# Two buffers for the transposed q and k of a differential-attention layer, its weights in pieces of 512 columns

## The chip, the cores and the metric

The kernel runs on one core of one Trainium2 chip. The metric is the device time of one execution in microseconds (us), the median of several runs. A profiled execution gives the trace from which all rows below are read; its time axis starts at the span's start.

## The reference

The program is a two-layer trunk on 640 tokens (128 of context, 512 of latents) of 1024 features. Layer 0 runs multi-head latent attention beside bidirectional retention. Layer 1 runs **differential attention** (4 heads) beside a bidirectional **RWKV-7** time mixing (8 heads). Each layer is followed by a gated convolutional feed-forward block. The part that matters here, cut to its core:

```python
# layer 1, differential half (h: normalised input, 640 x 1024)
q, k, v = h @ w_q, h @ w_k, h @ w_v          # 512 columns each
q = rope(rms_norm(q) * gain_q); k = rope(rms_norm(k) * gain_k)   # per head of 64; no rotation of the context tokens
k, v = concat(cached_k, k), concat(cached_v, v)
w = softmax(q1 @ k1.T) - lam * softmax(q2 @ k2.T)                # two maps per head
o = w @ v
# layer 1, RWKV half: for each of 640 tokens, forward and backward
state = state * decay - (state @ kk) (kk * a) + v k
```

## The kernel before, in words

The scan of the RWKV half (`rwkv_scan`, from about 1043 us to 1504 us of the span) is built from a main and a background stream. The main stream consists of `pre(g)` (the decays, gates and key products of a group of 128 tokens in each of the two directions: tiles `wp`, `lp`, `am`, `th`, `bp`, `sa`, `sb`, `kt`, `hq`, `L`), `lb(g)` and `lc(g)` (the inverse of the triangular matrices of group g, in DVE's line L1902 and its neighbours, with a round trip through DRAM at L1908 to L1917: `xd<-X`, then `X<-xd`), and `steps(g, d)` (the state updates, `pa`, `SV`, `yp`). The background stream is `side_mix`: `odd_qkv`, which makes the q, k and v of the differential layer, and after it `diff_attn`, the attention. `weave` (L241) advances the streams by a table of numbers when the program is written out. A scheduler then puts each engine's instructions into one fixed order by its own estimate of when each can start; that order is final, and every engine works it off in sequence.

`odd_qkv` runs through six groups of 256 columns: two of q, two of k, two of v. Each group needs 1 MB of weights, `w`, fetched on the SP queue by `load(g)` (L1311). Its products are five tiles of 128 tokens, eight matrix products each, at L1325: 240 instructions, 480 records in the trace since each is done in two passes. A q or k tile is post-processed one group later by `post` (L1277): DVE scales it (L1287), POOL applies the gain (L1288), DVE and POOL rotate it (L1293 to L1297), PE transposes it into the tile `qtr` (L1303), ACT and DVE split the transposed tile into two parts, `pt` (L440 and L444, called at L1305), and two DMAs on the SP queue carry `pt` to DRAM (L1307: `dq<-pt` for q, `dk<-pt` for k). There are 20 such tiles. The tile `pt` has one buffer, the weights have three buffers of 1024 columns. All tiles of `odd_qkv` come from one pool of fixed size. At the end the 512 KB of cached keys are loaded into one such weight buffer (L1347), split into two others, and written to `dk` (L1352); the attention reads `dk` afterwards.

The SP queue issues DMAs in its fixed order. Where a DMA needs data or a buffer that is not there yet, the queue stands at it, and what is behind it waits as well.

Of the kernel before, what the change touches and what calls it, by code (L numbers as in the profile page):

```python
# [9 lines left out]
F32 = mybir.dt.float32  # L10
F32R = mybir.dt.float32r
# [6 lines left out]
D = 1024  # L18
# [86 lines left out]
def _consts3():  # L105
    """Head sums land in rows 32 p + i; the selectors bring rows 32 p + i and 32 p + 2 + i back to half i of tile p."""
# [103 lines left out]
"""How the streams of the layers are woven: background steps in each part of the scan, spans of layer 0."""  # L210
# [3 lines left out]
LAG = 4  # L214


class Side:
    """A background stream: its matrix products are issued behind the main streams' product of LAG events before."""
# [22 lines left out]
def weave(bg, rate, *parts):  # L241
    """Advance several emission streams together; each (generator, begin, end) spreads evenly over [begin, end]."""
    ev = []
    for i, (g, b, e) in enumerate(parts):
        n = NSTEP[g.__name__]
# [17 lines left out]
class Trunk:  # L263
# [116 lines left out]
    def setup_late(self):  # L380
        """The loads that nothing needs before the first products."""
# [174 lines left out]
    def ada_half(self, c0):  # L556
        """Eight chunks of layer 0's modulation, from pieces that the queue brings in this order."""
# [30 lines left out]
    def norm_mod(self, side):  # L588
        """Layer 0: rstd and x * rstd do not wait for the modulation."""
# [26 lines left out]
    def norm_begin(self, l, which, pool):  # L616
        """Open the next norm: every final x[k] is scaled by the modulation and split at once, its rstd is applied after the
        matrix product; two more columns carry the shifts through it."""
# [19 lines left out]
    def norm_end(self, us, rb):  # L638
        """Close the norm: the first three products run while the rstd is being worked out."""
# [17 lines left out]
    def fm_norm(self, h, u, rb, ps=None):  # L657
        """One output tile of the normalised product, into the padded columns of u."""
# [104 lines left out]
    def head_sums(self, sqs, stat, mmt, tile):  # L763
        """Per-head sums of four tiles of squares: [tokens, (token tile, tile, half)]."""
# [16 lines left out]
    def head_rows(self, r, mmt, tile):  # L781
        """The [tokens, (token tile, tile, half)] columns as rows of hi and lo parts."""
# [16 lines left out]
    def head_bcast(self, rows, p, mmt):  # L799
        """Tile p of the rows, spread over the features of its two heads."""  # L800
# [134 lines left out]
    def mla_cached(self, kr, ccs, D):  # L935
        """Keys and values of the cache, before the first products."""
# [39 lines left out]
    def mla_rows(self, src, dst, tt, g, gain, D, tr):  # L976
        """Four heads of 128 tokens, turned to rows of features."""
# [288 lines left out]
    def odd_qkv(self, D):  # L1266
        """Differential q, k, v from the stored h: one 256-column group at a time, its post-processing one group behind."""
        nc, a = self.nc, self.a
        with self.pool("qk", 1, "left") as qp, self.psum("qps", 2) as qps, self.psum("qtr") as qtr:
# [41 lines left out]
            def load(g):  # L1311
                w = [tile("w", 1024, 3) for _ in range(2)]
                for i in range(2):
                    nc.sync.dma_start(w[i], a["wb_tm"][g][:, i * 1024:i * 1024 + 1024])
# [799 lines left out]
```

## Time and profile before

| what | us |
|---|---|
| median of three runs | 2073.32 |
| the three runs | 2075.4, 2061.55, 2073.32 |
| span of the profiled execution | 2059.5 |
| PE busy in it | 1952.7 (95%) |
| DVE busy in it | 1253.8 (61%) |
| ACT busy in it | 887.3 (43%) |

Of the profiled execution only the span is listed, no separate run time; the shortest run is 2 us longer than this span, the median 13.8 us. The stretch in which `odd_qkv` and the main stream of the scan run side by side is 1043 us to 1232 us. In the rows a name stands for a tile, `out<-in`; what stands in brackets behind a row, as [3.67 <-POOL th L1824], is how long the engine was idle before it and which instruction ended that.

### The profile page before, as it was taken

The numbers are of one execution on the slowest core, as the hardware profiler recorded it, in microseconds if no ns is written. First come the engines' busy times: TensorE is split into PE (matmuls) and PEld (weight loads), VectorE is DVE, ScalarE is ACT, GpSimd is POOL, SyncE is SP. The second block draws the span as 40 slices with busy tenths as digits, with TensorE's granted clock in tenths as the row PEclk, the third lists the DMA queues.
The fourth block names the chain that finished last, engine by engine and source line by source line (L and its number), as shares of the span: only waits on it lengthen the run. The fifth ranks groups of instructions, "written<-read, shape, count | busy, mean of one in ns | idle before, by whom it ended". The sixth has DMA issues, their size and how long they took to land.

```text
span 2059.5 us, 36275 instructions
## 1 busy us (share of the span) xinstructions
PE 1952.7 (95%) x14376; PEld 1765.7 (86%) x14376; DVE 1253.8 (61%) x2752; ACT 887.3 (43%) x1680; POOL 186.5 (9%) x365
## 2 busy tenths in 40 slices
PE   6999999999999999999989897898779999999999
PEld 3998565999899899999978676777679999999999
DVE  6554657556456465577436856877667764656555
ACT  4433344334244243456333334667534542524343
POOL 1001000000000000000024332332110000000000
PEclk9999999999999999999989998979989999999999
DMA  8237344234543512143264554454453212122221
GB/s 323 67 109 242 105 134 163 89 104 147 181 153 116 192 62 83 60 151 104 83 207 100 109 161 120 100 116 96 100 200 106 77 58 92 60 85 67 77 63 71
DMA packets 190676, 243.60 MB, mean 118 GB/s; under 512 B 90730, under 2 KB 132970, under 8 KB 190508
## 3 DMA queue, kind: packets, MB, share of 16 engines
q1 hardware_dynamic: 184880, 225.87, 35.7%
q0 software_dynamic: 3904, 13.37, 2.2%
q8 instruction: 113, 1.85, 0.4%
q10 hardware_dynamic: 1724, 2.06, 0.3%
q14 instruction: 55, 0.45, 0.1%
HBM read 202.05 MB, written 39.21 MB: 117 GB/s over the span
## 4 chain that ended last, share of the span: by engine, by line
PE 81%; DVE 7%; DMA 6%; ACT 3%; issue 2%; POOL 1%; SPq 0%; ACTq 0%; DVEq 0%; POOLq 0%
PE mm L470 59%; PE qkv L1325 2%; PE ada L541 2%; PE rv L913 1%; PE pv L1130 1%; PE mm L1097 1%; DMA dk<-pt 1%; PE ptr L1120 1%; PE sc L1442 1%; DVE X L1902 1%; DVE tmp L1901 1%; DMA xd<-X 1%; DMA mq<-tr 1%; DMA raw<-ada 1%; PE mm L1098 1%
## 5 line engine op out<-in xcount | busy, mean ns | idle before, releaser
L414 ACT CAST hi<-raw 128x1024 fp32r<-128x1024 f32 (+4 forms) x212 | 195.9, 925 | 574.1 <-PE mm L470 528.6
L470 PE MATMUL mm<-hhi,hi 128*128 128x322 f32 x1648 | 381.0, 312 | 0.0
L470 PE MATMUL mm<-hlo,hi 128*128 128x322 f32 x1648 | 380.3, 311 | 0.0
L470 PE MATMUL mm<-hhi,lo 128*128 128x322 f32 x1648 | 380.1, 311 | 0.0
L470 PEld LDWEIGHTS mm<-hhi,hi 128*128 128x128 f32 x1648 | 278.3, 189 | 8.7 <-issue 6.7
L470 PEld LDWEIGHTS mm<-hlo,hi 128*128 128x128 f32 x1648 | 279.5, 190 | 0.0
L470 PEld LDWEIGHTS mm<-hhi,lo 128*128 128x128 f32 x1648 | 278.6, 189 | 0.0
L415 DVE TENSOR_TENSOR lo<-raw,hi 128x1024 fp32r<-128x1024 f32 (+4 forms) x212 | 226.1, 1067 | 58.7 <-ACT hi L414 36.0
L672 DVE SCALAR_TENSOR_TENSOR x<-mm,ada,x 128x512 f32<-128x512 f32 (+1 forms) x176 | 88.7, 545 | 176.1 <-PE mm L470 175.9
L470 PE MATMUL mm<-ahi,hi 128*128 128x320 f32 x704 | 161.7, 311 | 0.0
L470 PE MATMUL mm<-ahi,lo 128*128 128x320 f32 x704 | 160.7, 309 | 0.0
L470 PE MATMUL mm<-alo,hi 128*128 128x320 f32 x704 | 160.3, 309 | 0.0
L663 DVE COPY shv<-mm 128x2 f32<-128x2 f32 x103 | 16.3, 159 | 207.9 <-PE mm L470 207.9
L470 PEld LDWEIGHTS mm<-ahi,hi 128*128 128x128 f32 x704 | 117.1, 188 | 12.0 <-ACT hi L414 10.1
L1325 PE MATMUL qkv<-w,x 128*128 128x256 f32 x480 | 118.9, 402 | 0.1
L470 PEld LDWEIGHTS mm<-ahi,lo 128*128 128x128 f32 x704 | 117.8, 188 | 0.0
L470 PEld LDWEIGHTS mm<-alo,hi 128*128 128x128 f32 x704 | 117.6, 188 | 0.0
L666 ACT ACTIVATE u<-u,shv 128x128 f32<-128x128 f32 (+1 forms) x176 | 90.3, 557 | 48.8 <-DVE u L665 47.0
L734 DVE SCALAR_TENSOR_TENSOR ac<-u,vt,ac 128x642 f32<-128x642 f32 x88 | 78.0, 887 | 52.5 <-ACT ac L732 52.3
L1325 PEld LDWEIGHTS qkv<-w,x 128*128 128x128 f32 x480 | 94.0, 201 | 17.0 <-issue 1.7
L732 ACT ACTIVATE ac<-u,vt 128x642 f32<-128x642 f32 x88 | 81.3, 925 | 2.8
L665 DVE TENSOR_TENSOR u<-mm,rb 128x128 f32<-128x128 f32 (+1 forms) x176 | 77.3, 481 | 2.5 <-ACT rb L650 2.5
(419 smaller groups left out, 3351.3 us busy)
## 6 DMA issues: line engine op xcount, KB each, us to landing
raw<-ada SPq DMA_DIRECT2D x96, 512.0 KB, 4.6
raw<-up SPq DMA_DIRECT2D x88, 512.0 KB, 3.5
raw<-down SPq DMA_DIRECT2D x32, 384.0 KB, 3.1
raw<-down SPq DMA_DIRECT2D x32, 320.0 KB, 2.8
fs<-df SPq DMA_DIRECT2D x10, 832.0 KB, 5.2
raw<-wb_fm SPq DMA_DIRECT2D x15, 512.0 KB, 3.5
w<-wb_tm SPq DMA_DIRECT2D x12, 512.0 KB, 4.5
raw<-wa_fm SPq DMA_DIRECT2D x11, 512.0 KB, 4.3
```

What stands on the lines that cost most here:

```text
L414: nc.scalar.copy(hi, t)
L415: nc.vector.tensor_tensor(lo, t, hi.bitcast(F32), op=OP.subtract)
L470: nc.tensor.matmul(ps[:, c0 + b:c0 + e], wt[:, ws], at[:, b:e], start=first and j == 0, stop=last and j == 2)
L541: nc.tensor.matmul(ps[32 * j:32 * j + 32, :], self.cs[:, k, :], pieces[j // 2][:, (j % 2) * 512:(j % 2) * 512 + 512], start=k == 0, stop=k ...
L665: nc.vector.tensor_tensor(u[:, o], ps[:, s], rb[:, s], op=OP.mult)
L666: nc.scalar.activation(u[:, o], u[:, o], AF.Identity, bias=sh[:, c:c + 1])
L672: nc.vector.scalar_tensor_tensor(x[:, s], ps[:, s], self.ada_v(l, part, m, c), x[:, s], op0=OP.mult, op1=OP.add)
L732: nc.scalar.activation(ac, u[:, 1:643], AF.Identity, scale=cv[:, 1, f:f + 1], bias=self.vec(f"cb{l}", f))
L734: nc.vector.scalar_tensor_tensor(ac, u[:, 0:642], cv[:, 0, f:f + 1], ac, op0=OP.mult, op1=OP.add)
L913: nc.tensor.matmul(ps[:, :272], at[:, ts], wt[:, k * 272:k * 272 + 272], start=n == 0, stop=n == 23)
L1097: nc.tensor.matmul(sc[:, 0:512], q, kT[:, 0:4], start=True, stop=True)
L1325: nc.tensor.matmul(ps, h[k][:, t * 128:t * 128 + 128], w[k // 4][:, k % 4 * 256:k % 4 * 256 + 256], start=k == 0, stop=k == 7)
```

## The change

The tile `pt` gets two buffers. To make room in the pool of unchanged size, the weights of a group come in four pieces of 512 columns (256 KB) in five buffers, where they came in two of 1024 (512 KB) in three. The product at L1325 picks the piece by `k // 2`. The cached keys are loaded, split and written in two halves of 512 columns, one behind the other. The pool's use is the same to the word: 3 x 1024 + 512 before, 5 x 512 + 2 x 512 after. Comments were removed as well, which changes no instruction. The core of the diff:

```diff
-                    pts = tile("pt", 512, 1, F32R).rearrange("p (n x) -> p n x", n=2)
+                    pts = tile("pt", 512, 2, F32R).rearrange("p (n x) -> p n x", n=2)
...
             def load(g):
-                w = [tile("w", 1024, 3) for _ in range(2)]
-                for i in range(2):
-                    nc.sync.dma_start(w[i], a["wb_tm"][g][:, i * 1024:i * 1024 + 1024])
+                w = [tile("w", 512, 5) for _ in range(4)]
+                for i in range(4):
+                    nc.sync.dma_start(w[i], a["wb_tm"][g][:, i * 512:i * 512 + 512])
                 return w
...
-                        nc.tensor.matmul(ps, h[k][:, t * 128:t * 128 + 128], w[k // 4][:, k % 4 * 256:k % 4 * 256 + 256], start=k == 0, stop=k == 7)
+                        nc.tensor.matmul(ps, h[k][:, t * 128:t * 128 + 128], w[k // 2][:, k % 2 * 256:k % 2 * 256 + 256], start=k == 0, stop=k == 7)
...
-            kc = tile("w", 1024, 3)
-            ks = [tile("w", 1024, 3, F32R) for _ in range(2)]
-            nc.sync.dma_start(kc, a["dkc"])
-            self.split_to(*ks, kc)
-            for i in range(2):
-                for c in range(2):
-                    for g in range(2):
+            for g in range(2):
+                kc = tile("w", 512, 5)
+                ks = [tile("w", 512, 5, F32R) for _ in range(2)]
+                nc.sync.dma_start(kc, a["dkc"][:, g * 512:g * 512 + 512])
+                self.split_to(*ks, kc)
+                for i in range(2):
+                    for c in range(2):
```

The scheduler lays out the engines' orders anew. PE has the same instructions; between the first product of `odd_qkv` and the products `lf` of L1943 of the first half of `lb(0)`/`lc(0)` their order differs, behind that it is nearly the same.

The first place is PE's order at the third `bp` (the product behind `th` of L1824, of the second group of `pre`). Numbers behind names count tiles. Before:

```order
L1303 MATMUL qtr_10931<-ident,raw_10705 128x128 x2
L1325 MATMUL qkv_10992<-w_10710,x_77 128x256
L1325 MATMUL qkv_10992<-w_10710,x_79 128x256
L1325 MATMUL qkv_10992<-w_10710,x_81 128x256
L1325 MATMUL qkv_10992<-w_10710,x_83 128x256
L1325 MATMUL qkv_10992<-w_10711,x_85 128x256
L1325 MATMUL qkv_10992<-w_10711,x_87 128x256
L1325 MATMUL qkv_10992<-w_10711,x_89 128x256
L1325 MATMUL qkv_10992<-w_10711,x_91 128x256
L1827 MATMUL bp_11296<-th_11267,rkb 32x128 x4
L1858 MATMUL sa_11344<-kr_11314,kb_11313 128x128 x4
L1859 MATMUL sb_11345<-kr_11314,kb_11313 128x128 x4
```

Now:

```order
L1325 MATMUL qkv_11232<-w_10960,x_77 128x256
L1325 MATMUL qkv_11232<-w_10960,x_79 128x256
L1325 MATMUL qkv_11232<-w_10961,x_81 128x256
L1325 MATMUL qkv_11232<-w_10961,x_83 128x256
L1325 MATMUL qkv_11232<-w_10962,x_85 128x256
L1325 MATMUL qkv_11232<-w_10962,x_87 128x256
L1325 MATMUL qkv_11232<-w_10963,x_89 128x256
L1325 MATMUL qkv_11232<-w_10963,x_91 128x256
L1303 MATMUL qtr_11148<-ident,raw_10955 128x128 x2
L1827 MATMUL bp_11320<-th_11291,rkb 32x128 x4
L1858 MATMUL sa_11368<-kr_11338,kb_11337 128x128 x4
L1325 MATMUL qkv_11260<-w_10960,x_77 128x256
```

Before, the product stands behind the 17th tile of products of `odd_qkv` and the transposes of the 10th tile of q and k; now it stands behind the 22nd tile of products and the 15th tile's transposes. The RWKV rows move back by 50 instructions there, the rows of `odd_qkv` move forward. From this pass's `wp` to its `bp` PE has 32 products of L1325 to do, where it had 24; from `bp` to the next `kt` 26, where it had 8.

The second place is PE's order at the fourth `wp` (the start of `pre(1)`'s second direction). Now:

```order
L1325 MATMUL qkv_11500<-w_11162,x_81 128x256
L1325 MATMUL qkv_11500<-w_11162,x_83 128x256
L1303 MATMUL qtr_11360<-ident,raw_11085 128x128 x2
L1791 MATMUL wp_11517<-wup_10315,wx_10343 128x512
L1325 MATMUL qkv_11500<-w_11163,x_85 128x256
L1325 MATMUL qkv_11500<-w_11163,x_87 128x256
L1303 MATMUL qtr_11428<-ident,raw_11123 128x128 x2
L1800 MATMUL lp_11528<-c_3608,lw_11519 128x128 x4
L1815 MATMUL am_11546<-fs_11272,aup 128x128 x4
L1325 MATMUL qkv_11500<-w_11164,x_89 128x256
L1325 MATMUL qkv_11500<-w_11164,x_91 128x256
```

Before:

```order
L1303 MATMUL qtr_11032<-ident,raw_10804 128x128 x2
L1873 MATMUL kt_11479<-ident,kb_11313 128x64 x4
L1873 MATMUL kt_11479<-ident,kb_11381 128x64 x4
L1791 MATMUL wp_11493<-wup_10315,wx_10343 128x512
L1325 MATMUL qkv_11108<-w_10710,x_77 128x256
L1325 MATMUL qkv_11108<-w_10710,x_79 128x256
L1325 MATMUL qkv_11108<-w_10710,x_81 128x256
L1325 MATMUL qkv_11108<-w_10710,x_83 128x256
```

The chain `wp`, `lp`, `am` stood in the fourth group of products and now stands in the sixth, the last; a product on that group's third piece, `w_11163`, now stands between `wp` and `lp`. From this `wp` to its `bp` there are 6 products of L1325, where there were 24.

The third place is the SP queue where the inverse of `lb(0)` makes its round trip (`xd`, `zd`, `X`, `zb`). Before:

```order
L1314 DMA w_10945<-wb_tm 128x1024
L1909 DMA xd_11591<-X_11286 128x32x16
L1908 DMA zd_11592<-ZI_11589 128x16x32
L1314 DMA w_11141<-wb_tm 128x1024
L1307 DMA dk<-pt_11076 64x4x128 x2
L1917 DMA X_11599<-xd_11591 32x2x256 x2
L1913 DMA zb_10336<-zd_11592 32x16x32 x4
```

Now:

```order
L1909 DMA xd_11615<-X_11310 128x32x16
L1908 DMA zd_11616<-ZI_11613 128x16x32
L1314 DMA w_11162<-wb_tm 128x512
L1338 DMA dv<-raw_11422 128x256
L1917 DMA X_11623<-xd_11615 32x2x256
L1307 DMA dk<-pt_11238 64x4x128
L1314 DMA w_11163<-wb_tm 128x512
L1307 DMA dk<-pt_11238 64x4x128
L1314 DMA w_11164<-wb_tm 128x512
```

Before, the first half of the last group's weights, `w_11141`, stood ahead of the reload `X<-xd`, and its second half 12 rows behind it. Now the second piece stands ahead of the first `X` DMA, the third and the fourth, `w_11163` and `w_11164`, right behind it, with a `dk<-pt` before each. Further up in the queue the second half of `LI<-ld`, the input of `lb(0)`, now stands behind the DMAs of the tenth `pt`; before, both halves stood ahead of the seventh's.

## Rows read from the trace of the kernel before

**Rows 1.** The page: span, engines' busy time, the products of L1325 (busy, mean ns | idle before).
```profile
span 2059.5 us, 36275 instructions
...
PE 1952.7 (95%) x14376; PEld 1765.7 (86%) x14376; DVE 1253.8 (61%) x2752; ACT 887.3 (43%) x1680; POOL 186.5 (9%) x365
...
L1325 PE MATMUL qkv<-w,x 128*128 128x256 f32 x480 | 118.9, 402 | 0.1
```

**Rows 2.** Waits from 1043 to 1240 us: total us, times, longest.
```profile
ACT pt L440 <- DMA dq<-pt: 13.9, 6, 3.7
ACT pt L440 <- DMA dk<-pt: 13.0, 5, 4.0
```

**Rows 3.** Chain of waits from 1043 to 1240 us: shares, one piece.
```profile
by line: PE qkv L1325 24.2%; DMA dk<-pt 12.9%; issue 7.6%; DMA dq<-pt 5.8%; DVE X L1902 3.6%; DVE tmp L1901 3.2%; SPq L1307 2.6%; DVE pt L444 2.5%; ACT pt L440 2.3%; PE wp L1791 2.1%; PE kt L1873 2.0%; DVE kb L1849 1.9%; DVE raw L1287 1.9%;
...
1064.75 7.10 PE qkv L1325 x32
```

**Rows 4.** Timeline of ACT: two of the 20 pt splits, the steps' first SV.
```profile
1101.08 0.37 ACT L440 CAST pt<-qtr 128x256 fp32r<-128x256 f32 x1 [3.68 <-DMA dq<-pt]
...
1140.57 0.37 ACT L440 CAST pt<-qtr 128x256 fp32r<-128x256 f32 x1 [2.33 <-DMA dq<-pt]
...
1232.71 0.78 ACT L1982 ACTIVATE SV<-pa 64x256 f32<-64x256 f32 x2 [0.78 <-PE pa L1980]
```

**Rows 5.** Windows of 20 us: busy us by engine, then PEclk, DMA share, GB/s.
```profile
1080.00:1100.00 20.00, 19.95 (x132) 16.23 (x129) 10.86 (x27) 6.55 (x17) 8.87 (x12) 1.00 0.13 27
...
1140.00:1160.00 20.00, 11.98 (x73) 9.49 (x71) 19.72 (x55) 5.04 (x13) 9.83 (x12) 0.83 0.22 63
1160.00:1180.00 20.00, 20.00 (x98) 16.78 (x97) 13.30 (x43) 9.33 (x24) 4.89 (x10) 0.91 0.72 126
...
1200.00:1220.00 20.00, 18.39 (x188) 13.95 (x189) 5.39 (x19) 7.13 (x19) 0.96 (x3) 0.87 0.52 126
```

**Rows 6.** Timeline of PE around its two longest pauses and at L1943.
```profile
1137.40 0.44 PE L1303 MATMUL qtr<-ident,raw 128*128 128x128 f32 x2 [0.78 <-DVE pt L444]
1137.68 3.62 PE L1325 MATMUL qkv<-w,x 128*128 128x256 f32 x16
1144.96 0.43 PE L1827 MATMUL bp<-th,rkb 128*32 128x128 f32 x8 [3.67 <-POOL th L1824]
...
1147.33 5.00 PE L1325 MATMUL qkv<-w,x 128*128 128x256 f32 x16
...
1154.30 0.41 PE L1303 MATMUL qtr<-ident,raw 128*128 128x128 f32 x2 [0.75 <-DVE raw L1297]
...
1159.17 1.12 PE L1873 MATMUL kt<-ident,kb 64*128 64x64 f32 x8 [3.60 <-DVE hq L1863]
1160.21 5.16 PE L1325 MATMUL qkv<-w,x 128*128 128x256 f32 x15
...
1211.10 0.60 PE L1943 MATMUL lf<-zb,tt 32*32 32x32 f32 x26
```

**Rows 7.** Timeline of the SP queue: issue start, issue time.
```profile
1125.96 1.13 SPq L1887 DMA_DIRECT2D LI<-ld  x2
...
1169.69 0.39 SPq L1909 DMA_DIRECT2D xd<-X  x1
...
1177.52 1.27 SPq L1917 DMA_DIRECT2D X<-xd  x2
...
1248.25 0.38 SPq L1909 DMA_DIRECT2D xd<-X  x1
```

**Rows 8.** DMA issues from 1040 to 1250 us: count, KB each, median to landing.
```profile
w<-wb_tm SPq DMA_DIRECT2D x12, 512.0 KB, 4.5
...
dk<-pt SPq DMA_DIRECT2D x20, 128.0 KB, 2.6
...
LI<-ld SPq DMA_DIRECT2D x4, 256.0 KB, 4.2
...
w<-dkc SPq DMA_DIRECT2D x1, 512.0 KB, 5.8
```

More of the change, by code (lines that the diff above doesn't have):

```diff
@@ L1344, in odd_qkv @@
                 w = wn
-            kc = tile("w", 1024, 3)
-            ks = [tile("w", 1024, 3, F32R) for _ in range(2)]
-            nc.sync.dma_start(kc, a["dkc"])
-            self.split_to(*ks, kc)
-            for i in range(2):
-                for c in range(2):
-                    for g in range(2):
+            for g in range(2):
[5 more added lines that the diff above has]
+                    for c in range(2):
                         nc.sync.dma_start(D["k"][g, c, 2 * i:2 * i + 2, :, 5:7].rearrange("h d t k -> d h (t k)"),
-                                          ks[i][64 * c:64 * c + 64, g * 512:g * 512 + 512].bitcast(F32).rearrange("p (h x) -> p h x", h=2))
+                                          ks[i][64 * c:64 * c + 64].bitcast(F32).rearrange("p (h x) -> p h x", h=2))
             yield
```

## The prediction, made before the changed kernel was run

> **What bounds the kernel now.** I read the page first. PE is busy for 1952.7 us, 95% of a span of 2059.5 us [rows 1]. So whatever the change does, it counts only where PE itself stands still or runs at its lower clock. The buffer in question is seen next, in the waits of the stretch in which it is used. ACT, which writes the first half of `pt`, waits 13.9 us for the landing of `dq<-pt` and 13.0 us for that of `dk<-pt`, eleven waits in all [rows 2]. ACT's timeline shows what such a wait is: the split could begin, but the only buffer is still being read by the DMA, which takes 2.6 us from issue to landing [rows 4, 8]. In this stretch's own chain of waits those landings stand with 12.9% and 5.8% [rows 3]. That looks like 26.9 us to be had. The reader should now ask who waits for ACT.
>
> The windows answer. In 1080 to 1100 us PE is busy for 19.95 of 20 us, though the most of ACT's wait of 3.68 us lies inside, and in 1160 to 1180 us for 20.00 [rows 4, 5]. Between one `pt` and the next, PE has the products of L1325 to do: 32 records in 7.10 us, or 0.222 us each, so the 480 records are some 106 us [rows 3]. They cover most of the waits. PE stands still in one window only, 1140 to 1160 us, with 11.98 us busy, where DVE is full with 19.72 us; a smaller loss is in 1200 to 1220 us, with 18.39 us [rows 5]. PE's timeline gives the two long pauses: 3.67 us before `bp`, until POOL's `th`, and 3.60 us before `kt`, until DVE's `hq` [rows 6]. Neither of them is a wait for `pt`; both belong to the RWKV stream, whose DVE work is in the same queue as the work on q and k. After each pause the granted clock is at the lower level for a while: PEclk is 0.83 and 0.91 in these two windows and 1.00 before [rows 5], and 16 products take 5.00 us where 16 took 3.62 us just ahead [rows 6].
>
> **The change, part by part.** *The second `pt` buffer* removes the eleven waits on ACT. By itself that gives PE nothing where it is full. What it moves is the order: the rows of `odd_qkv` go forward, those of `pre` back. From the `wp` of the pass with the first pause to its `bp` PE now has 32 products, where it had 24: eight more, of two records each, 3.6 us, the length of the pause. From there to the `kt` with the second pause it has 26 where it had 8, 8.0 us more against a pause of 3.60 us. I take both as gone, and two short ones between them, before transposes that waited for DVE: 3.67 + 3.60 + 0.78 + 0.75 = 8.8 us. The half-clock products go with them: 5.00 - 3.62 = 1.38 us for the 16 after the first pause, and 5.16 - 15 x 0.222 = 1.83 us for the 15 after the second [rows 3, 6]. Together that is **12 us gained**. The bounds: nothing, if the pauses turn up at another place, since DVE's work is the same; and 16 us, if PE has no pause left at all, which is 8.0 + 1.6 us of idle time in the two windows and the clock's missing shares, 0.17 x 12 + 0.09 x 20 + 0.13 x 18.4 = 6.2 us [rows 5].
>
> *What is late next.* Since `pre` now runs later and `odd_qkv` earlier, two new waits can come. The first is on the last group's weights. On the SP queue the third and fourth piece stand behind the reload `X<-xd`, which waits until the result of `lb(0)` has been in DRAM. In the trace `xd` is issued at 1169.69 us and `X` at 1177.52 us, 7.8 us later, and the queue stands for that time [rows 7]. One `dk<-pt` issue follows, so the third piece is issued about 1.2 us after `X` and lands by the row of the nearest size, 256 KB in 4.2 us [rows 8], that is some 13 us after `xd`. PE wants it before `lp` of the last `pre` pass. When is that? The `lf` of L1943 stands at 1211.10 us [rows 6]; less 12 us it is at 1199 us; between lie 20 products of 0.444 us, 8.9 us, and about as much of the RWKV stream's (an estimate, from its rows in the same place before), so PE is there at about 1181 us. With `xd` as before the piece lands at 1183 us, and PE waits 2 us. But `lb(0)` begins later: the second half of its input, issued at 1125.96 us before [rows 7], now stands behind the tenth `pt`, which was split at 1140.57 us [rows 4], at best some 2.3 us earlier without its wait. So the input comes up to 12 us later. DVE is freer by then, because work on q and k has been done early, and I take `xd` to be 3 us later: 1173 us, the piece at 1186 us, and **5 us lost**. The bounds are 0 (`xd` 2 us earlier) and 8.4 us (`xd` 6.5 us later).
>
> The second is the last pass of `pre(1)`. From its `wp` to its `bp` PE had 24 products and now has 6, so 18 fewer, 8.0 us, cover the work of ACT, POOL and DVE between the two. The trace shows no place with so few; the bounds are 0 and these 8.0 us, and the nearest row is the 3.67 us pause before the `bp` that had 24 [rows 6], at a place where DVE was full. Here DVE was only 13.30 us busy in 1160 to 1180 us [rows 5], and a part of that work goes on while PE waits for the weights. I take **3 us lost**.
>
> *The pieces of weights.* The twelve loads become 24. SP spends about 0.4 us on each further issue, as on `xd` [rows 7], 4.8 us in all, in a stretch of 190 us in which the queue mostly stands at waits: nothing. The products of L1325 were idle-free in the trace, 0.1 us in 480, so none waits for `w` [rows 1]; pieces free their buffer sooner than halves did. A quarter lands at 4.2 us against 4.5 us for a half [rows 8], so it costs nothing unless it is asked for late, which is counted above. The Trainium skill ("DMA: Bandwidth & Descriptors", section "Bandwidth") speaks against this part: it wants transfers of 1 MiB and more, and its section "Anatomy of one DMA — SWDGE (gpsimd) path" gives each DMA a fixed part of about 2 us. By the Trainium skill the extra twelve loads would be 24 us if nothing else covered them; the rows here have them beside full PE windows, so the sum leaves that out and it stands below as a rival.
>
> *The cached keys in halves.* The second half can be loaded only when the first half's chain of split and write is under way, and on ACT its cast now stands ahead of the first `SV` of the steps. One load is 5.8 us [rows 8]; about 3 us of such a round trip could hold up `SV`, at worst. The cover is `lb(1)` on DVE: the first `SV` stands at 1232.71 us and the next round trip's `xd` is issued at 1248.25 us, 15.5 us later [rows 4, 7]. I take 0; without that cover the whole 3 us would count; the bounds are 0 and 3 us, since nothing can be gained by it.
>
> The sum is 12 - 5 - 3 - 0 = **4 us gained**. Against the profiled span: 2059.5 - 4 = 2055.5 us. The median of the runs is 13.8 us above that span, so I forecast 2073.3 - 4 = 2069 us.
>
> **The rivals.**
> - *All of the DMA waits come off the end.* For it speaks the stretch's chain, where these landings are 18.7% [rows 3]; against it, PE's full windows [rows 5]. It gives 26.9 us [rows 2]: 2046 us. 6%.
> - *PE's pauses go and nothing takes their place.* For it: more products ahead of the two paused rows, and a piece that comes in time if `xd` is 2 us earlier, as PE runs ahead. It gives the upper bound of 16 us: 2057 us. 19%.
> - *Slower: the SP queue holds the last pieces.* The mechanism is the one priced at 5 us above, at its bound: `xd` 6.5 us later, the third piece at 1189 us, PE idle for 8.4 us before `lp`, and 1.8 us at the lower clock behind it as after the second pause [rows 6]; with it the last pass of `pre(1)` is late (3 us) and the keys' second half ahead of `SV` costs its 3 us. 12 - 8.4 - 1.8 - 3 - 3 = -4.2: 2078 us. With these other losses the sum turns negative from the point where PE waits 4.2 us, with `xd` some 2 us later than before. For it: the later input of `lb(0)`, and a queue that stands for 7.8 us at this very place [rows 7]. Against it: DVE has 6.7 us free in the window 1160 to 1180 us [rows 5]. 19%.
> - *The change doesn't do what it says.* ACT's waits go, but the pauses only move, because DVE's sum of work in 1140 to 1160 us (19.72 us) is done at another time and PE waits for it there: 0 us, 2073 us. 12%.
> - *The smaller loads are late as such.* If two quarters follow one another rather than overlap, a half's worth lands 2 x 4.2 - 4.5 = 3.9 us later [rows 8]. At the last two groups, where pieces are asked for as they land, that is 8 us against the gain of 4: 2077 us. No wait for `w` in the trace bears it out [rows 1]. 4%. The Trainium skill's rule on small transfers would show itself so.
>
> My forecast has the remaining 40%.
>
> **How the numbers follow.** About 1%, some 21 us, is what a measurement of this kernel can tell from no change; the three runs alone lie 14 us apart. Faster by over 1% means under 2053 us: most of the first rival, and the second's better end, 0.10. Slower by over 1% means over 2094 us: only the bounds of several losses together, 0.05. Within 1%: 0.85. The range from 2051 to 2083 us holds the forecast, the second to fifth rivals and some of the scatter of the runs; below it lies the first rival, above it the slower one's tail.
>
> **What would show it.** In the profile of the changed kernel, ACT's waits for `dq<-pt` and `dk<-pt` should be near nothing. PE's pauses before the third `bp` and its `kt` should be gone, and the window 1140 to 1160 us full. A new pause of some 5 us should stand before the product on the third piece of the last group, near 1181 us, ended by a DMA of `w`, and `X` of the round trip should be issued near 1181 us. The `lf` of L1943 should stand near 1207 us, not 1211 us, and everything behind it the same few us earlier. The forecast is wrong if that `lf` is no earlier, or if it is earlier and the scan still ends where it did.

## The result, and the profile after

The changed kernel is slower: 2082.49 us in the median of eleven runs against 2067.41 us, a ratio of **1.0062 with a 95% interval from 1.0034 to 1.0089**, or 7 to 18 us; the two medians alone lie 15 us apart. The forecast was 4 us faster. The profiled execution has a span of 2077.4 us, 17.9 us more than that of before, and its busy times are much the same: PE 1960.6 us.

Not all of the 17.9 us belongs to the change. PE's timeline, whose rows are start, duration, instruction, has the same row at 1038.01 us before and at 1046.16 us after, ahead of everything that the change touches; layer 0's instructions and their order are the same in both. Before:

```profile
1038.01 2.32 PE L1534 MATMUL mm<-v,gup 128*128 128x320 f32 x8
...
1054.56 2.07 PE L1325 MATMUL qkv<-w,x 128*128 128x256 f32 x4
...
1218.89 2.08 PE L1791 MATMUL wp<-wup,wx 65*128 65x512 f32 x2
```

After:

```profile
1046.16 2.32 PE L1534 MATMUL mm<-v,gup 128*128 128x320 f32 x8
...
1063.64 2.93 PE L1325 MATMUL qkv<-w,x 128*128 128x256 f32 x6
...
1235.09 1.12 PE L1791 MATMUL wp<-wup,wx 65*128 65x512 f32 x2
```

So 8.15 us came in layer 0. They are scatter of single executions: the first product of `odd_qkv` stands at 1054.56 and 1060.96 us in two traces of before, at 1063.64 and 1058.53 us in two of the changed kernel. To be free of it, every trace below is measured from its own first product of `odd_qkv` (L1325). The fifth `wp`, the first row of `pre(2)`, stands right behind the stretch that the prediction is about. To it the kernel before takes 1218.89 - 1054.56 = **164.3 us**, the changed one 1235.09 - 1063.64 = **171.4 us**. From there to the end of the span it is 840.6 and 842.3 us. A second trace of each gives 162.0 and 171.6 us to the fifth `wp`, 843.8 and 847.7 us behind it. The stretch thus repeats within 2.3 us, and the change costs 7 to 10 us in it; behind it, the two traces of one kernel differ by as much as the two kernels. The rest of the 7 to 18 us of the timed runs is not placed by these traces.

One window per kernel over that stretch (length, PE busy, the other engines, PEclk, DMA share, GB/s) shows in what form the 7 us are lost. Before, then after:

```profile
1054.60:1218.90 164.30, 153.06 (x952) 123.98 (x951) 100.25 (x291) 60.55 (x162) 55.42 (x83) 0.95 0.49 117
```

```profile
1063.60:1235.10 171.50, 158.16 (x952) 125.74 (x951) 102.54 (x286) 59.44 (x162) 57.62 (x83) 0.92 0.44 112
```

PE does the same work, 952 records (a product of L1325 leaves two). It is idle for 13.3 us where it was 11.2 us, and busy for 158.2 us where it was 153.1 us: 2 us are lost in pauses, 5 us in the products themselves, at a granted clock of 0.92 instead of 0.95. The waits of the changed kernel from 1043 to 1260 us (total us, times, longest) answer to [rows 2]:

```profile
ACT pt L440 <- DMA dq<-pt: 4.6, 2, 3.6
PE qtr L1303 <- DVE pt L444: 4.4, 2, 3.9
...
PEld qkv L1325 <- DMA w<-wb_tm: 3.6, 1, 3.6
PE qkv L1325 <- DMA w<-wb_tm: 3.4, 1, 3.4
PE bp L1827 <- POOL th L1824: 3.4, 1, 3.4
```

ACT's waits for the landing of `pt` fell from 26.9 to 4.6 us, as the buffer promises. PE has three waits in place of the two of before. PE's timeline, which answers to [rows 6]:

```profile
1157.31 0.66 PE L1303 MATMUL qtr<-ident,raw 128*128 128x128 f32 x2 [3.90 <-DVE pt L444]
1157.76 6.16 PE L1325 MATMUL qkv<-w,x 128*128 128x256 f32 x16
...
1198.12 2.08 PE L1325 MATMUL qkv<-w,x 128*128 128x256 f32 x4 [3.42 <-DMA w<-wb_tm]
1200.66 0.66 PE L1303 MATMUL qtr<-ident,raw 128*128 128x128 f32 x2 [0.46 <-DVE pt L444]
1201.11 1.91 PE L1791 MATMUL wp<-wup,wx 65*128 65x512 f32 x2
1202.82 1.91 PE L1325 MATMUL qkv<-w,x 128*128 128x256 f32 x4
...
1213.70 0.43 PE L1827 MATMUL bp<-th,rkb 128*32 128x128 f32 x8 [3.40 <-POOL th L1824]
1214.05 3.68 PE L1325 MATMUL qkv<-w,x 128*128 128x256 f32 x8
```

The pauses before the third `bp` and its `kt` are gone. In their place stands one of 3.90 us before a transpose, one of 3.42 us before products on the last group's second piece, and one of 3.40 us before the fourth `bp`. By the order of the new kernel the four records at 1198.12 us, ahead of `wp`, are on the second piece, `w_11162`; those on the third, behind `wp` at 1202.82 us, have no pause. The second traces have the same pauses: 3.93, 3.38 and 3.31 us in the changed kernel, 3.67 and 3.60 us in that of before. Behind each of the new ones PE runs at the lower level of its clock, as windows show (length, PE busy, PEclk, DMA share, GB/s):

```profile
1157.80:1161.00 3.20, 3.20 (x9) 0.50 0.68 129
1198.20:1206.00 7.80, 7.34 (x19) 0.50 0.90 219
1214.10:1217.60 3.50, 3.50 (x12) 0.51 0.99 276
```

In the rows above, 16 records take 6.16 us, where [rows 6] have 3.62 us, and 8 take 3.68 us, or 0.46 us each where a record takes 0.222 us at the upper level [rows 3].

Where these pauses come from is seen on the queue and on DVE. The SP queue, which answers to [rows 7]:

```profile
1144.84 0.49 SPq L1887 DMA_DIRECT2D LI<-ld  x1
1145.43 1.24 SPq L1307 DMA_DIRECT2D dq<-pt  x2
1146.71 0.61 SPq L1887 DMA_DIRECT2D LI<-ld  x1
...
1190.46 0.37 SPq L1909 DMA_DIRECT2D xd<-X  x1
...
1193.76 1.54 SPq L1314 DMA_DIRECT2D w<-wb_tm  x1
...
1195.88 0.64 SPq L1917 DMA_DIRECT2D X<-xd  x1
1196.61 0.60 SPq L1307 DMA_DIRECT2D dk<-pt  x1
1197.30 0.55 SPq L1314 DMA_DIRECT2D w<-wb_tm  x1
```

Counted from the first product, `LI<-ld` is issued 81.2 and 83.1 us behind it, where it was 71.4 us, and `xd` at 126.8 us, where it was 115.1 us: `lb(0)` runs 10 to 12 us later. The second piece of the last group is the `w` issued at 1193.76 us: it stands behind `xd` in the queue, so it waits for the end of `lb(0)`, and PE starts on it at 1198.12 us. The third piece, behind `X`, is the `w` at 1197.30 us.

On DVE `lb(0)` isn't shorter than before, it is later. Its first and last row on DVE before:

```profile
1130.71 0.19 DVE L1901 TENSOR_TENSOR tmp<-LI,X 128x31 f32<-128x31 f32 x1 [2.50 <-DMA LI<-ld]
...
1168.90 0.17 DVE L1902 TENSOR_TENSOR X<-X,tmp 128x16 f32<-128x16 f32 x1
```

And after, with the work on q and k between:

```profile
1151.73 0.19 DVE L1901 TENSOR_TENSOR tmp<-LI,X 128x31 f32<-128x31 f32 x1 [1.57 <-DMA LI<-ld]
...
1156.06 0.26 DVE L1902 TENSOR_TENSOR X<-X,tmp 128x100 f32<-128x100 f32 x1
1156.24 0.42 DVE L1293 TENSOR_TENSOR m<-raw,ropd 128x256 f32<-128x256 f32 x1
1156.58 0.25 DVE L1901 TENSOR_TENSOR tmp<-LI,X 128x96 f32<-128x96 f32 x1
1156.74 0.42 DVE L444 TENSOR_TENSOR pt<-qtr,pt 128x256 fp32r<-128x256 f32 x1
...
1190.26 0.17 DVE L1902 TENSOR_TENSOR X<-X,tmp 128x16 f32<-128x16 f32 x1
```

That is 38.4 us before and 38.7 us after. DVE's half of `pt`, which frees the tile `qtr`, stands behind the first rows of `lb(0)`, and those wait for `LI`. PE's next transpose waits for that `pt`: the 3.90 us. `lb(0)` shared DVE with the work on q and k before as well; what differs is what PE has to do between the two transposes. Before, then after:

```profile
1133.21 0.44 PE L1303 MATMUL qtr<-ident,raw 128*128 128x128 f32 x2
...
1134.22 1.99 PE L1325 MATMUL qkv<-w,x 128*128 128x256 f32 x8
```

```profile
1152.65 0.38 PE L1303 MATMUL qtr<-ident,raw 128*128 128x128 f32 x2
1152.96 0.45 PE L1976 MATMUL yp<-hq,SV 128*64 128x64 f32 x6
```

Before, eight records of products lie between, and the pause ahead of the next transpose is 0.78 us [rows 6]; after, none does.

### The profile page after: what moved, and what is told of

Read it like the earlier page. It is cut to its first block, busy times and chain, and to the rows that moved or that the text cites. A ratio compares the mean times of both kernels' runs of the same rounds, so it can differ in the third digit from the quotient of the medians.

```text
span 2077.4 us, 36287 instructions
## 1 busy us (share of the span) xinstructions
PE 1960.6 (94%) x14376; PEld 1767.6 (85%) x14376; DVE 1250.5 (60%) x2753; ACT 884.2 (43%) x1681; POOL 192.0 (9%) x365
## 4 chain that ended last, share of the span: by engine, by line
PE 81%; DMA 8%; DVE 5%; ACT 3%; issue 1%; SPq 1%; POOL 1%; DVEq 0%; ACTq 0%; POOLq 0%
PE mm L470 59%; PE qkv L1325 3%; PE ada L541 2%; PE rv L913 2%; PE pv L1130 1%; PE mm L1097 1%; PE ptr L1120 1%; DMA LI<-ld 1%; DMA xd<-X 1%; PE sc L1442 1%; DVE tmp L1901 1%; DVE X L1902 1%; PE yp L2002 1%; PE mm L1098 1%; DMA X<-xd 1%
## 5 line engine op out<-in xcount | busy, mean ns | idle before, releaser
L1325 PE MATMUL qkv<-w,x 128*128 128x256 f32 x480 | 123.1, 409 | 4.4 <-DMA w<-wb_tm 3.4
L1325 PEld LDWEIGHTS qkv<-w,x 128*128 128x128 f32 x480 | 94.1, 203 | 22.1 <-DMA w<-wb_tm 3.6
```

The source lines that it names most:

```text
L1325: nc.tensor.matmul(ps, h[k][:, t * 128:t * 128 + 128], w[k // 2][:, k % 2 * 256:k % 2 * 256 + 256], start=k == 0, stop=k == 7)
```

## The experiments

The question was which part of the change moved the work. Theory A: **the order**. The weights' smaller loads let the scheduler put the products of `odd_qkv` further ahead of `pre`, and the later `pre` and `lb(0)` cost the time. Theory B: the second `pt` does it, by crowding DVE and the SP queue. Theory C: the keys' round trip costs it. Theory D: pieces are late as such, whatever the order. Later, for what is lost behind the fifth `wp`: F, the reshuffled order there; G, the pieces or the second `pt`.

The table has every run: products of L1325 ahead of the second, third and fourth `wp` in PE's order; us from the first product to the fifth `wp`, and from there to the end of the span, in one trace; and the ratio to the kernel before over the timed runs. Ahead of the fifth `wp` the kernel before has 228 products. e9, e12, e13, e14 and e16 have 2, 10, 6, 6 and 6 fewer, e10 has 12 more and e15 2 more, 0.444 us each: by so much their stretch is shorter or longer for work that only moved behind it or ahead of it.

| kernel | ahead of wp 2, 3, 4 | to fifth wp | rest | ratio, interval |
|---|---|---|---|---|
| before (two traces) | 64, 112, 152 | 164.3; 162.0 | 840.6; 843.8 | 1 |
| changed (two traces) | 72, 144, 204 | 171.4; 171.6 | 842.3; 847.7 | 1.0062 (1.0034 to 1.0089) |
| e1 pieces and halves, one pt | 72, 136, 184 | 181.0 | 846.1 | 1.0100 (1.0068 to 1.0132) |
| e2 second pt only | 64, 112, 144 | 159.9 | 846.2 | 1.0043 (1.0014 to 1.0071) |
| e3 control of e2 | 64, 112, 152 | 164.3 | 843.0 | 1.0009 (0.9983 to 1.0035) |
| e6 loads split, buffers of before | 72, 136, 192 | 176.7 | 845.3 | 1.0102 (1.0060 to 1.0145) |
| e7 keys in halves only | 64, 112, 152 | 162.2 | 843.1 | 0.9995 (0.9970 to 1.0021) |
| e10 before, order as in the change | 72, 136, 176 | 179.0 | 855.2 | 1.0138 (1.0112 to 1.0164) |
| e5 change, four piece buffers | 64, 112, 144 | 164.4 | 861.0 | 1.0091 (1.0058 to 1.0123) |
| e8 as e5, keys ahead | 64, 112, 144 | 165.3 | 846.5 | 1.0069 (1.0039 to 1.0099) |
| e9 change, table 80, 32, 103 | 64, 112, 152 | 162.8 | 850.9 | 1.0061 (1.0039 to 1.0083) |
| e12 change, table 80, 28, 107 | 64, 112, 152 | 159.2 | 862.8 | 1.0076 (1.0049 to 1.0103) |
| e13 change, table 80, 30, 105 | 64, 112, 152 | 158.8 | 842.2 | 1.0018 (0.9992 to 1.0044) |
| e14 change, table 78, 32, 105 | 64, 112, 144 | 157.7 | 845.2 | 0.9977 (0.9954 to 1.0000) |
| e15 before, table 89, 25, 101 | 64, 112, 152 | 163.9 | 841.1 | 1.0036 (1.0014 to 1.0059) |
| e16 as e14, keys ahead | 64, 112, 144 | 155.9 | 847.1 | 0.9979 (0.9947 to 1.0012) |
| e17 change, keys ahead | 72, 144, 204 | 173.4 | 841.8 | 1.0035 (1.0001 to 1.0069) |

### One part alone

e1, the change without its second `pt`:

```diff
-                    pts = tile("pt", 512, 2, F32R).rearrange("p (n x) -> p n x", n=2)
+                    pts = tile("pt", 512, 1, F32R).rearrange("p (n x) -> p n x", n=2)
```

> The change without the second pt buffer: weights in pieces of 512 columns, cached keys in halves, pt one buffer. From the first product of L1325 to the second block of lf at L1943 the kernel before takes 163.3 us and the changed one 170.8 us. Theory A (the pieces move the order of PE: the products of odd_qkv come forward and the last pass of pre is left without cover): 168 to 173 us here, and the whole 5 to 12 us slower than before. Theory B (the second pt buffer does it, since q and k's work comes early and crowds DVE and the SP queue): 162 to 165 us here, the whole within 3 us of before. Theory C (only the cached keys' round trip costs): 163 us to that point, and 5 us lost behind it.

It is slower than the change itself: 181.0 us to the fifth `wp`, 180.0 us to the second block of `lf`, more than A had said. B falls. PE's timeline has four pauses of 2 us or more before the fourth `bp`'s, of which three are ended by the work on q and k:

```profile
1126.69 0.50 PE L1303 MATMUL qtr<-ident,raw 128*128 128x128 f32 x2 [4.66 <-DVE raw L1297]
...
1166.08 3.72 PE L1325 MATMUL qkv<-w,x 128*128 128x256 f32 x16 [2.00 <-ACT m L1333]
...
1182.47 4.63 PE L1325 MATMUL qkv<-w,x 128*128 128x256 f32 x10 [2.99 <-ACT m L1333]
...
1207.78 5.15 PE L1325 MATMUL qkv<-w,x 128*128 128x256 f32 x14 [2.22 <-DMA w<-wb_tm]
...
1218.01 0.65 PE L1827 MATMUL bp<-th,rkb 128*32 128x128 f32 x8 [4.87 <-POOL th L1824]
```

The tile `pt` has one buffer again, and ACT waits 22.1 us for its landings. One of these waits stands right ahead of the `m` that ends the pause of 2.99 us; that the others come from `pt` isn't shown:

```profile
1181.49 0.37 ACT L440 CAST pt<-qtr 128x256 fp32r<-128x256 f32 x1 [5.79 <-DMA dk<-pt]
```

So the loads' pieces lose 17 to 19 us of this stretch, and the second buffer on top of them wins 9.6 us back. It moves the order further as well, from 184 to 204 products ahead of the fourth `wp`, so the 9.6 us belong to both.

e2, the second `pt` alone, and e3, its control; the room comes from two tiles of the steps:

```diff
-... "ys": (256, 2), "yv": (256, 2)}
+... "ys": (256, 1), "yv": (256, 1)}
...
-                    pts = tile("pt", 512, 1, F32R).rearrange("p (n x) -> p n x", n=2)
+                    pts = tile("pt", 512, 2, F32R).rearrange("p (n x) -> p n x", n=2)
```

> The kernel before with a second pt buffer and nothing else in that stretch; the room comes from the tiles ys and yv of the steps, which get one buffer in place of two (they are first used behind that stretch). Theory A: the order of PE stays nearly that of before, so 158 to 163 us from the first product of L1325 to the second block of lf (163.3 before), ACT's 26.9 us of waits for dq and dk below 8 us. Theory B: 168 to 173 us. Theory C: 163 us.

> The kernel before with one buffer for ys and yv, the control for the run with a second pt buffer. All theories: 163 to 164 us to the second block of lf, as before, since its order of instructions there is the same; behind that 0 to 6 us lost in the steps, which the run with two pt buffers shares.

e3 repeats the 164.3 us. e2 nearly keeps the order, with 8 products fewer ahead of the fourth `wp`, and takes 159.9 us, 2 to 4 us less, as A has it; ACT's waits for the landing of `pt` are gone. The whole doesn't gain: its runs are 0.4% above before, those of its control 0.1%. Its late order is not that of its control, as is told below. e4 is the repeat of before, in the table.

> The kernel before once more, for the scatter of its stretches: 162 to 165 us from the first product of L1325 to the second block of lf at L1943 (163.3 in the trace before), and the 8 us by which the profile of the changed kernel was late before its first product of L1325 as scatter of the DMAs of layer 0.

e6 leaves buffers, `pt` and keys as they were and only issues two DMAs for each weight buffer:

```diff
-                    nc.sync.dma_start(w[i], a["wb_tm"][g][:, i * 1024:i * 1024 + 1024])
+                    for j in range(2):
+                        nc.sync.dma_start(w[i][:, j * 512:j * 512 + 512], a["wb_tm"][g][:, i * 1024 + j * 512:i * 1024 + j * 512 + 512])
```

> The kernel before, each 1024-column weight buffer filled by two DMAs of 256 KB in place of one of 512 KB; buffers, pt and keys as before. The order of PE moves as in the changed kernel: 72, 136, 192 products ahead of the second, third and fourth wp. Theory A: 171 to 182 us from the first product of L1325 to the fifth wp, the whole 8 to 22 us slower. Rival E (the buffers' size and number, or the keys in halves, cost the time): 162 to 165 us, the whole as before.

That alone moves PE's order and costs 1%: the size of the loads is enough, and the buffers' number needn't change for it. (Part of the 1% may lie behind the stretch, as is told below.) e7 has the keys in halves alone (the change's loop over `kc` and `ks`, with slices of the old buffers):

> The kernel before with the cached keys loaded, split and written in two halves one behind the other, and nothing else; the order of PE up to there is that of before. Theory A: 162 to 165 us to the fifth wp; the first SV of the steps 4 to 10 us later than the 178.2 and 172.8 us of before (188.0 in the changed kernel), and 0 to 6 us of the whole. Theory C (the keys' round trip is the main cost): 8 us or more of the whole.

The keys cost nothing: ratio 0.9995, and the first `SV` stands 173.0 us behind the first product, no later than in the two traces of before (178.2 and 172.8). I had expected 4 to 10 us later. C falls.

### The order alone, in both directions

The table `BG` says how many background steps go with each part of the scan. Its first three numbers set the order without touching the size of a buffer or a DMA. e10 gives the kernel before an order like that of the pieces in e1 and e6 (first pair of lines), e9 gives the whole change the order of before (second pair):

```diff
-BG = (89, 24, 102, 0, 22, 72, 0)
+BG = (105, 24, 86, 0, 22, 72, 0)
...
-BG = (89, 24, 102, 0, 22, 72, 0)
+BG = (80, 32, 103, 0, 22, 72, 0)
```

> The kernel before with 105, 24, 86 in BG: buffers, pieces, pt and keys as before, PE's order like that of the pieces: 72, 136, 176 products ahead of the second, third and fourth wp. It has 240 products ahead of the fifth wp (228 before), 12 more of 0.444 us, 5.3 us. Theory A: LI<-ld near 81 to 88 us, xd<-X near 127 to 139 us, the fifth wp at 175 to 190 us and the whole 8 to 20 us slower than before. Rival D: LI<-ld at 71 to 76 us, xd<-X at 115 to 120 us, the fifth wp at 168 to 170 us, the whole within 5 us of before.

> The changed kernel, all of it, with the first three numbers of the weaving table BG at 80, 32, 103 (89, 24, 102 before; the sum is the same), which gives PE nearly the order of before: 64, 112, 152, 226 products of L1325 ahead of the second to fifth wp (before 64, 112, 152, 228; changed 72, 144, 204, 228). Theory A (the order): 158 to 163 us from the first product of L1325 to the fifth wp, LI<-ld issued near 71 us behind that product and xd<-X near 116 us (before 71 and 115, changed 81 and 127), and the whole from 4 us faster to 6 us slower than before. Rival D (the smaller pieces and halves cost it by themselves): 168 us or more, and the whole 8 us or more slower.

Over the stretch, e10 then e9:

```profile
1058.90:1237.90 179.00, 163.89 (x978) 132.50 (x977) 103.99 (x283) 60.39 (x162) 63.03 (x94) 0.92 0.47 122
```

```profile
1059.80:1222.60 162.80, 153.43 (x948) 122.99 (x947) 99.83 (x291) 59.85 (x162) 55.21 (x83) 0.95 0.48 116
```

e10 with the old buffers and loads takes 179.0 us at a clock of 0.92, with `LI<-ld` at 87.2 us and `xd` at 136.4 us; even less the 5.3 us for its 12 extra products that is 9 to 12 us over before. It has the same pause as e1, at nearly the same place:

```profile
1124.26 0.41 PE L1303 MATMUL qtr<-ident,raw 128*128 128x128 f32 x2 [4.67 <-DVE raw L1297]
```

e9 has all of the change and takes 162.8 us at 0.95, as before, with `LI<-ld` at 72.5 us and `xd` at 117.9 us. **In this stretch the order is the cause, and D falls.** But the whole of e9 is as slow as the change, 1.0061, which I had not expected. e12 says the same, and e11 is the repeat of the changed kernel:

> The changed kernel with 80, 28, 107 in BG: 64, 112, 152, 218 products ahead of the second to fifth wp, so ten fewer than before ahead of the fifth. Theory A: 154 to 160 us from the first product of L1325 to the fifth wp, LI<-ld near 71 us, xd<-X near 116 us, the whole from 8 us faster to 6 us slower than before. Rival D: 164 us or more, and the whole 8 us or more slower than before.

> The changed kernel once more, for the scatter of its stretches: all theories 169 to 174 us from the first product of L1325 to the fifth wp (171.4 in its first trace), with pauses of 2 to 5 us before the product on the last group's third piece, and before the fourth bp.

e5 and e8 came to it from another side, with four buffers of 512 columns (e8 also with the keys' loads ahead, the second half in a buffer of its own, the part behind the dots):

```diff
-                w = [tile("w", 512, 5) for _ in range(4)]
+                w = [tile("w", 512, 4) for _ in range(4)]
...
+            kcs = [tile("w", 512, 4), tile("kc", 512, 1)]
+            for g in range(2):
+                nc.sync.dma_start(kcs[g], a["dkc"][:, g * 512:g * 512 + 512])
```

> The changed kernel with four buffers of 512 columns for the weights in place of five; second pt buffer, pieces and halves of the keys stay. With four buffers a group's pieces can be asked for only as the group before is used up, and the order of PE is near that of before: 64, 112, 144 products of L1325 ahead of the second, third and fourth wp (before 64, 112, 152; changed 72, 144, 204). Theory A (the order, with products of odd_qkv far ahead of pre, costs the time): 158 to 164 us from the first product of L1325 to the fifth wp (164.3 and 162.0 in two traces of before, 171.4 changed, 181.0 with pieces alone), and the whole within 4 us of before. Rival D (smaller transfers and more issues on the SP queue are late as such, whatever the order): 169 us or more, since there are as many pieces and fewer buffers.

> As the run with four pieces, and both halves of the cached keys are loaded at once, the second into a buffer of its own, which the room left by the fifth piece allows; so the second half's split no longer waits for a load behind the first half's writes. Theory A: to the fifth wp as with four pieces; the first SV within 3 us of before; the whole 0 to 6 us faster than the run with four pieces, so 0 to 8 us faster than before. If the keys' round trip hides behind lb(1), no difference from the run with four pieces.

Both keep the stretch, at 164.4 and 165.3 us, and lose behind it, where I had expected e5 within 4 us of before and e8 up to 8 us faster. With four buffers the same small loads leave the order near that of before: it takes both the smaller loads and the room for them to move it.

### Behind the fifth wp

In e5, e8, e9 and e12 the scheduler had laid out the scan's end anew as well. Set side by side with the order of before, PE's 12004 matrix instructions differ behind the fifth `wp` in some 1300 to 1500 lines (an instruction that moved counts at both places), against some 300 in the changed kernel. The same holds of e2 with some 1400, against 100 in its control, and of e6 and e10 with 1400 and 1600, so what these three lose in the whole need not come from the stretch alone. e13 and e14 are tables with which the change has both parts near the order of before; e15 moves one background step in the kernel before, so that only the end is reshuffled. The three new lines are those of e13, e14 and e15:

```diff
-BG = (89, 24, 102, 0, 22, 72, 0)
+BG = (80, 30, 105, 0, 22, 72, 0)
+BG = (78, 32, 105, 0, 22, 72, 0)
+BG = (89, 25, 101, 0, 22, 72, 0)
```

> The changed kernel with 80, 30, 105 in BG: 64, 112, 152, 222 products ahead of the second to fifth wp, and behind the fifth wp some 310 of PE's instructions stand elsewhere than before (some 1320 in the run with 80, 32, 103, 280 in the changed kernel). Theory F (the reshuffled late order costs 7 to 19 us): the fifth wp at 158 to 162 us behind the first product, the first ohi product of the output 286 to 298 us behind the fifth wp (291 to 295 in four traces of the order of before), the whole from 8 us faster to 4 us slower than before. Rival G (the pieces or the second pt cost it late): 301 us or more there, and the whole 10 us or more slower.

> The changed kernel with 78, 32, 105 in BG: 64, 112, 144, 222 products ahead of the second to fifth wp, some 250 of PE's instructions elsewhere behind the fifth. Theory F: as the run with 80, 30, 105: the fifth wp at 156 to 162 us, the first ohi product 286 to 298 us behind it, the whole from 8 us faster to 4 us slower. Rival G: 301 us or more, the whole 10 us or more slower.

> The kernel before with 89, 25, 101 in BG: one step of the background stream is moved by a place in the table; pieces, buffers and pt as before. PE's order is that of before up to the fifth wp (two more products there), and behind it some 1370 instructions stand elsewhere. Theory F: the fifth wp at 162 to 166 us, the first ohi product 298 to 315 us behind it, the whole 5 to 18 us slower than before. Rival G: 291 to 296 us there, the whole within 4 us of before.

From the fifth `wp` to the first `ohi` product e13 takes 293.0 us and e14 296.5 us, as F had it (e9 has 302.3 us, e12 313.6 us), and the whole change is then level with before: 1.0018 and 0.9977. G falls. Over all kernels whose order in the stretch is near that of before, the timed runs part as F says: with the late order laid out anew (e2, e5, e8, e9, e12, e15) the ratios are 1.0036 to 1.0091, each interval above 1; with both orders near (e3, e7, e13, e14, and e16 below) they are 0.9977 to 1.0018, each interval reaching 1. e15 is 0.4% slower in its twelve runs, which fits F, but its one trace has only 290.1 us there, which doesn't. A single trace can't settle that end: the two traces of the kernel before, windows of 310 us from the fifth `wp`, show PE's clock at 0.85 and 0.81 with the same instructions, and 261 and 271 us busy:

```profile
1218.90:1528.90 310.00, 261.14 (x3069) 214.62 (x3065) 218.28 (x674) 180.48 (x450) 85.98 (x154) 0.85 0.51 130
```

```profile
1223.00:1533.00 310.00, 270.68 (x3050) 222.15 (x3048) 214.28 (x672) 179.86 (x449) 81.70 (x151) 0.81 0.52 128
```

Last, the keys' loads ahead of both splits, in the change (e17) and with the table of e14, which leaves 44 instructions elsewhere (e16):

```diff
+            kcs = [tile("w", 512, 5) for _ in range(2)]
+            for g in range(2):
+                nc.sync.dma_start(kcs[g], a["dkc"][:, g * 512:g * 512 + 512])
             for g in range(2):
-                kc = tile("w", 512, 5)
                 ks = [tile("w", 512, 5, F32R) for _ in range(2)]
-                nc.sync.dma_start(kc, a["dkc"][:, g * 512:g * 512 + 512])
-                self.split_to(*ks, kc)
+                self.split_to(*ks, kcs[g])
```

> The changed kernel with both halves of the cached keys loaded at once, ahead of the first split; the table BG and PE's order up to the fifth wp as in the changed kernel. Theory A: the fifth wp at 170 to 173 us (171.4 and 171.6), the first SV some 6 us earlier than 188.0 and 187.3 us, and the whole 0 to 5 us faster than the changed kernel, so still 6 to 15 us slower than before. If the keys' round trip were the main cost, the whole would be within 3 us of before.

> The changed kernel with 78, 32, 105 in BG and both halves of the cached keys loaded at once, ahead of the first split. 64, 112, 144, 222 products ahead of the second to fifth wp; behind the fifth wp 44 of PE's instructions stand elsewhere than before. Theory F: the fifth wp at 156 to 161 us behind the first product, 839 to 848 us from there to the end of the span (840.6 to 843.8 in four traces with before's late order), the whole 3 to 9 us faster than before. Rival G (the pieces or the second pt cost it late): 849 us or more, the whole slower.

e17's 1.0035 can't be told from the change's 1.0062; its first `SV` is 2 to 3 us earlier, where I had expected 6 us. e16 has the shortest stretch of all, 155.9 us, 6 to 8 us under before, of which 2.7 us are its six products that now stand behind the stretch. The whole is 0.9979, with an interval that takes in 1; from the first product to the end of the span its trace has 1003.0 us, those of before 1004.9 and 1005.8 us. e14 and e16 are the best versions found, and neither is surely faster than the kernel before.

```profile
1059.50:1215.40 155.90, 148.68 (x939) 118.96 (x938) 101.27 (x291) 60.40 (x161) 54.84 (x83) 0.97 0.50 121
```

## Why the prediction was wrong

**"12 us gained"** is the term that failed, and with it the step that 12 us of pauses would go because products stand ahead of the paused rows. The two pauses named did go, and the two short ones. But `pre` and `lb(0)`, which the moved products hold up, still have all their work to do, and the pauses came at other places: 3.90 us before a transpose, where DVE was at `lb(0)` and PE had no product left in its order. PE's idle time is 13.3 us instead of 11.2 us. The prediction took `xd` to be 3 us later, because DVE would be freer by then; it is 11.7 us later, and `lb(0)` takes 38.7 us on DVE where it took 38.4 us. The lower bound of the term, nothing, and the rival of pauses that only move had this mechanism, at 0 us. The sign that the prediction gave itself says the same: the `lf` that was to come 4 us earlier stands at 164.2 us from the first product, where it was at 156.5 us [rows 6].

```profile
1227.84 0.69 PE L1943 MATMUL lf<-zb,tt 32*32 32x32 f32 x32
```

**"What it moves is the order"** was said of the second `pt`. That is the wrong part of the change. With `pt` alone (e2) the order in the stretch is nearly that of before; with the loads alone (e6) it moves; `pt` on top of the pieces moves it further (e1 against the change). The prediction gave the pieces 0 us, because no product waits for `w`. They are no wait, they are a cause: how the loads are cut decides, with the buffers there are for them, how far the products go ahead. The 256 KB pieces land in a median of 3.8 us, the 512 KB halves landed in 4.5 us, and with the order held near that of before the 24 loads cost nothing that the timings can tell (e13, e14). The Trainium skill ("DMA: Bandwidth & Descriptors", sections "Bandwidth" and "Anatomy of one DMA — SWDGE (gpsimd) path") speaks against small transfers; its fixed part of about 2 us is fitted to DMAs that GpSimd issues, and SP issues these loads. By the prediction's estimate from it, 24 us if nothing covers them, e13 and e14 would be slower by 1%; the intervals end at 0.4% and at 0, so that price isn't seen here.

**"5 us" and "3 us" lost** came out as pauses of 3.42 us and 3.40 us. The second was right in place and cause. The first was near in size by luck: the prediction had the third piece late behind the reload `X`, and it is the second piece that is late, behind `xd` itself. What was missing is the lower clock behind the new pauses. The prediction took away the half-clock products of the old pauses, 3.2 us, and added none for the new ones, save in its slower rival. Over the stretch PE is busy 5.1 us longer for the same products.

**The slower rival** named the right queue and sign, and nearly the number: 2078 us, where the change's 13 us on the prediction's own base of 2073 us would be 2086 us. It rested on the third piece and on `xd` 6.5 us later; `xd` was 11.7 us later, but PE itself came later, the third piece held up nothing, and the pause is 3.4 us, not 8.4 us.

**What bounds the kernel** was right in the main: PE's pauses and its clock behind them. ACT's 26.9 us of waits went to 4.6 us, and the whole was slower. That the second buffer gives PE nothing by itself was too strong: the stretch of e2 is 2 to 4 us shorter.

**The keys** at 0 us were right (e7). **The order behind the scan's first part** was taken as unchanged. It is nearly so in the change, whose rest is 842.3 and 847.7 us against 840.6 and 843.8 us; in the variants with that order laid out anew it is where the gain is lost again. Which rows there cost the time was not found.

With both orders held near those of before, the change (e13, e14) and the change with the keys ahead (e16) lie between 4 us slower and 5 us faster: 1.0018, 0.9977, 0.9979. All three intervals reach no change, so the forecast's 4 us are neither shown nor excluded.

## What to carry to other kernels

Where a scheduler lays out the order, a change of a load's size or of a buffer's number is first a change of the order; hold the order (here with one table) before crediting the change with a gain or a loss. A background stream that runs further ahead is no gain where the main stream's chain sets the end: it takes the cover from the chain's last links and lays their work on an engine that is then busy. And a pause of PE cost its length and the lower clock behind it in these traces, a new one as well as an old one.

## What the runs showed that was not expected

Executions of one program differ in layer 0 already: at the first product of `odd_qkv` the traces lie between 1054.6 and 1064.6 us, with the same instructions ahead of it. Between the first traces of before and after the 8.15 us arise in several steps within the first 371 us and stay constant from there to 1038 us. What makes the steps isn't shown. It is enough to hide a gain of 4 us in a pair of profiles, and a stretch measured from its own first row leaves it out.
